# Pinning SyncE to the written plan, and leaving the instructions behind the second plan to the scheduler

## The chip, the cores and the metric

The kernel runs on one core of one Trainium2 chip. Five queues of instructions are spoken of: PE (TensorE matmuls; PEld are its weight loads), DVE (VectorE), ACT (ScalarE), POOL (GpSimd) and SP (SyncE, which in this kernel issues nearly every DMA transfer). The metric is the device time of one execution in microseconds (us); smaller is better. Each queue works through its own instructions strictly in the order in which the program holds them, and an instruction that waits for a semaphore holds all those behind it on its queue.

## The reference, cut to what matters

One decoder layer on x of 1024 tokens x 1024 columns in float32, with two inputs to one output projection and a gated feed-forward part with a short convolution:

```python
h = rms_norm(x, norm1_g)
q, k, v, glu_a, glu_b = split(h @ w_in)                 # 512 columns each
attn = stick_breaking_attention(rms(q), rms(k), v)      # 8 heads x 64
c = causal_depthwise_conv(glu_a * sigmoid(glu_b), conv_dw_w, conv_dw_b)   # 31 taps
c = silu(layer_norm(c))
x = x + concat([attn, c]) @ w_out
h = rms_norm(x, norm2_g)
gate, val = split(h @ w_up)                             # 2816 columns each
gate = silu(causal_depthwise_conv(gate, ffn_dw_w, ffn_dw_b))              # 3 taps
x = x + (gate * val) @ w_down
```

## The kernel before, in words

Everything is float32. A product of two float32 matrices is made of three matmuls (`mm3`, L386 to L389): each operand is split into a high part, a cast by ACT (L383), and a low part, a subtraction by DVE or POOL (L384 in `split`), and high x high (L387), high x low (L388) and low x high (L389) are summed in one PSUM bank. So before PE can start a product, ACT has to write the high part of a weight and another engine its low part.

The work has four stages, laid one over the other. First the input projection and the convolution module (until about 200 us of the profile), then the attention (about 200 to 400), then the output projection, the second norm and the transposed activations for the feed-forward part (until about 490), then `w_up` in 22 blocks of 128 gate and 128 value columns (until about 900) and `w_down`. Each `w_up` block f takes seven products instead of eight: the four quarters of its weights (a11, a12, a21, a22) and of the activations (b11, b21, b22) are combined into sums with the names S1 to S4 and T1 to T4, and the products 11·11, 12·21, S2·T2, S3·T3, S1·T1, S4·22 and 22·T4 are added up. A product is 12 matmuls over 512 columns, so a block is 84 matmuls.

For block f, `load_up(f)` has SP load two weight tiles (`rawu`, L1805, 512 KB each), and `sums_up(f)` makes the operands: POOL adds and subtracts quarters (s1 in L1829, a21 in L1830, a11 in L1831, a12 in L1835), ACT and DVE split the seven results. `up(f)` makes the products, adds them into the gate and value rows `gv` on DVE, makes the three-tap convolution (ACT L2009, two DVE operations L2011), the silu (ACT L2013) and the product with the value rows (DVE L2014), and has SP store the result (L2015, `act_d`).

What sets the order of the instructions: up to block 0 of `w_up`, the work is recorded as steps of a `Plan`, and `plan.run(ORDERS[0])` and `plan.run(ORDERS[1])` emit the steps in the order of two tables of numbers. The first table covers the work up to the attention and the output projection, the second the second norm, the transposes with the sums T1 to T4 (`both`, L1749 to L1751, and d1 to d4, L1783 to L1788) and the products of block 0 (`first_operands`, L1860 to L1947, among them L1885 for the low parts and L1928 for the sums into `gv`). A scheduler behind the kernel lays out all emitted instructions on the five queues by its own estimate of times. It keeps the emitted order only where `in_order` (L465) has tied each instruction of an engine to the one before it on that engine; the engines for which this is done are listed in `ORDERED` (L41): PE, DVE, ACT and POOL. SP is not among them, so the place of each DMA issue is the scheduler's choice.

`in_order` is called behind each of the two plans, and a third time in the loop over the blocks (L2023, when f is 0): there it also ties, on DVE, ACT and POOL, everything that was emitted by `load_up(1)`, `up(0)` and `sums_up(1)`, in the order in which the code is written. In that written order, the convolution, silu and gate product of block 0 come before the operands of block 1. Behind that the scheduler is free.

The names in the program have a number at the end that counts tiles; `aS_1_5097`, `aS_1_5100`, `aS_1_5103` and `aS_1_5107` are the parts of S2, S1, S3 and S4 of block 1, `a_1_5110` that of a22, `y_5086` is the gate of block 0, `aS_0_5018` is S4 of block 0 and `bT_4408` is T4.

Of the kernel before, what the change touches and what calls it, by code (L numbers as in the profile page):

```python
# [37 lines left out]
LN_AT = 190.0  # L38
PAIRS = [3, 2, 2, 2, 2]
AHEAD = 4  # L40
ORDERED = (mybir.EngineType.PE, mybir.EngineType.DVE, mybir.EngineType.Activation, mybir.EngineType.Pool)  # L41
AHEAD_Z, AHEAD_SCAN = 1.4, 0.5
QK_FROM, QK_TO = -3.0, 7.0
CONV_FROM, CONV_TO = 8.0, 31.0
# [100 lines left out]
class Plan:  # L145
# [36 lines left out]
    def add(self, cost, *args):  # L182
        if not isinstance(cost, dict):
            cost, args = {cost: args[0]}, (lambda eng, f=args[1]: f(),) + args[2:]
        op = Plan.Op()
        op.shares = "DVE2" in cost
        op.cost, op.emit, op.key = {e.rstrip("2"): c for e, c in cost.items()}, args[0], args[1]
        op.after = list(args[2]) if len(args) > 2 else []
        op.takes = list(args[3]) if len(args) > 3 else []
        op.end, op.engine, op.n, op.moves = None, None, len(self.ops), [Plan.ROWS]  # L190
        self.ops.append(op)
        return op
# [77 lines left out]
def kernel(  # L270
# [21 lines left out]
    nc = tc.nc  # L292
# [169 lines left out]
    def part_of(big_tile, i, words):  # L462
        return big_tile[:, i * words:(i + 1) * words]

    def in_order(start_at, last=None, engines=ORDERED):  # L465
        last = {} if last is None else last
        for ins in nc.cur_bb.bb.instructions[start_at:]:
            if ins.engine in engines:
                if ins.engine in last:
                    tc.add_manual_dep(ins, last[ins.engine].name, mybir.DependencyInfo(  # L470
                        mybir.DependencyClass.NoSync, mybir.DependencyReason.DATA), reason="planned order")
                last[ins.engine] = ins
        return last

    start_at = len(nc.cur_bb.bb.instructions)
    g1 = []
# [796 lines left out]
    for h, half in [(h, half) for h in range(H) for half in range(2)]:  # L1273
# [38 lines left out]
        for g in (2 * half, 2 * half + 1):  # L1312
# [47 lines left out]
            last = None  # L1360
            if g % 2 == 0:
                po, pd = plan.token("o"), {}
            for sp in range(g + 1):
# [50 lines left out]
                last = add("PE", 480, products, k, [c] + v2 + ([last] if last else [prev_last] if g % 2 else []))  # L1414
# [203 lines left out]

    plan.run(ORDERS[0])
    in_order(start_at)  # L1620
    conv_ctx.close()
    ps_ctx.close()
# [18 lines left out]
    start_at = len(nc.cur_bb.bb.instructions)  # L1641
# [154 lines left out]
    def load_up(f):  # L1796

        both = []
        for b in (0, DFF):
            if f == 1 and b == 0:  # L1800
                both.append(next_raw[0])
                continue
            both.append(op.tile([P, ND, P], F32, tag="xt", name=f"rawu{f}_{b}", bufs=3) if f % 2 else
                        raw([P, ND, P], F32, f"rawu{f}_{b}"))
            nc.sync.dma_start(both[-1], w_up_k[:, :, b + f * P:b + (f + 1) * P])  # L1805
        return both
# [177 lines left out]
    gv, banks_of, A_next, next_raw = [], {}, {}, []  # L1984
    first_operands(FIRST)
    plan.run(ORDERS[1])
    last_planned = in_order(start_at)
    start_at = len(nc.cur_bb.bb.instructions)

    def up(f, A):  # L1990
        def product(a, b):
# [25 lines left out]
    for f in range(NF):  # L2017
        if f + 1 < NF:
            raw_next = load_up(f + 1)
        up(f, A)  # L2020
        if f + 1 < NF:
            A = sums_up(f + 1, raw_next)
        if f == 0:  # L2023
            in_order(start_at, last_planned, ORDERED[1:])

# [117 lines left out]
    for i in range(len(PAIRS)):  # L2145
        for n, name in enumerate(using if i else making):
# [7 lines left out]
            for s in range(4):  # L2154
# [4 lines left out]
                for j, ((ah, al), (bh, bl)) in enumerate(parts):  # L2159
                    first, last = begins and j == 0, j == len(parts) - 1  # L2160
# [42 lines left out]
```

## Time and profile before

| | |
|---|---|
| median of 3 runs | 1114.94 us (1114.22 to 1115.05) |
| the profiled execution | 1115.21 us |
| its span in the trace | 1112.9 us |
| PE busy | 1088.1 us (98%) |
| DVE, ACT, POOL busy | 78%, 53%, 52% of the span |
| moved by DMA | 118.00 MB, 106 GB/s on average |

The span is the part of an execution between the first and the last instruction in the trace; 2.3 us of the profiled execution lie around it. Rows of the timeline read: start in us, duration in us, engine, line, operation, output<-input, shapes, how many were taken together, and in brackets the idle time of the engine before it and what ended that. Rows of the view of waits read: engine, output and line that waited, the releaser, total us, how many times, the longest. Rows of the windows read: the stretch, its length, then the busy time and number of instructions of PE, PEld, DVE, ACT and POOL, the clock granted to PE as a share of full speed, the share of the DMA engines' time and the GB/s moved.

### The profile page before, as it was taken

To read this page: it belongs to the slowest core of one execution; us is meant where nothing else is said; L and a number is where in the kernel's file an instruction comes from. 1 tells how busy PE (TensorE), PEld (TensorE's weight loads), DVE (VectorE), ACT (ScalarE), POOL (GpSimd) and SP (SyncE) were. 2 spreads that over 40 slices of the span, in tenths; PEclk is the share of its full clock that TensorE was granted. 3 is DMA by queue.
4 is the path that set the end of the run, shared out by engine and by line. 5 is a ranking of instruction groups with operands and counts; after the bars stand their busy time and mean duration, and the time that the engine had idled before them with its cause. 6 is when DMAs were issued, how large, how long until landed. Compare 5 with 4: busy or idle time off the path is not lost.

```text
span 1112.9 us, 14818 instructions
## 1 busy us (share of the span) xinstructions
PE 1088.1 (98%) x5258; PEld 905.4 (81%) x5258; DVE 871.7 (78%) x1200; ACT 586.9 (53%) x1050; POOL 580.6 (52%) x496
## 2 busy tenths in 40 slices
PE   8999999999999999979999999999999999999998
PEld 5888878889898887857888888888888888888887
DVE  5488798789989886878876777677777678797785
ACT  6445466676766654734433434333333378676660
POOL 3177889874734324753433133223322189888770
PEclk9999999999999999998999999999999999999999
DMA  7121210343732434522322222213132482403404
GB/s 269 39 57 32 82 58 20 114 152 120 238 87 77 142 122 144 171 57 78 112 79 92 77 95 75 96 62 107 59 96 75 149 324 77 150 21 133 152 2 150
DMA packets 110504, 118.00 MB, mean 106 GB/s; under 512 B 21369, under 2 KB 90208, under 8 KB 110430
## 3 DMA queue, kind: packets, MB, share of 16 engines
q1 hardware_dynamic: 110414, 117.06, 32.0%
q8 instruction: 41, 0.67, 0.3%
q14 instruction: 33, 0.27, 0.1%
q10 hardware_dynamic: 16, 0.00, 0.0%
HBM read 82.43 MB, written 28.31 MB: 100 GB/s over the span
## 4 chain that ended last, share of the span: by engine, by line
PE 86%; POOL 4%; DVE 3%; DMA 3%; ACT 2%; issue 2%; SPq 0%; DVEq 0%; POOLq 0%; ACTq 0%
PE dn L2162 19%; PE u_S L387 7%; PE u_S L388 7%; PE u_S L389 7%; PE u L387 5%; PE u L389 5%; PE u L388 5%; PE po L1403 3%; PE wT L1375 3%; PE qk L387 3%; PE qk L389 3%; PE qk L388 3%; POOL attn L879 2%; PE z L1334 2%; PE z L1335 1%
## 5 line engine op out<-in xcount | busy, mean ns | idle before, releaser
L2162 PE MATMUL dn<-wd,wd 128*128 128x512 f32 x768 | 181.4, 389 | 0.0
L2162 PEld LDWEIGHTS dn<-wd,wd 128*128 128x128 f32 x768 | 144.2, 188 | 29.9
L387 PE MATMUL u_S<-bT,aS 128*128 128x512 f32 x264 | 103.9, 393 | 10.4 <-ACT aS L383 10.4
L388 PE MATMUL u_S<-bT,aS 128*128 128x512 f32 x264 | 103.4, 392 | 0.0
L389 PE MATMUL u_S<-bT,aS 128*128 128x512 f32 x264 | 102.8, 390 | 0.0
L2165 DVE TENSOR_TENSOR c<-dn,c 128x512 f32<-128x512 f32 x120 | 81.5, 686 | 26.7 <-PE dn L2162 26.1
L2067 ACT CAST wd<-rawd 128x512 fp32r<-128x512 f32 x128 | 72.5, 619 | 32.8 <-DMA rawd<-act_d 9.5
L383 ACT CAST aS<-rawu 128x512 fp32r<-128x512 f32 x63 | 38.8, 621 | 93.2 <-PE u_S L389 66.9
L1356 DVE TENSOR_TENSOR_SCAN nb<-nb,one 128x128 f32<-128x128 f32 (+7 forms) x64 | 84.6, 1340 | 0.6 <-ACT nb L1342 0.5
L1829 POOL TENSOR_TENSOR s<-rawu 128x512 f32<-128x512 f32 x21 | 28.8, 1370 | 107.6 <-DMA rawu<-in_w_up_dram 80.8
L2066 ACT COPY whole<-rawd 128x512 f32<-128x512 f32 x110 | 63.4, 586 | 24.2 <-DVE wd L2068 11.6
L1835 POOL TENSOR_TENSOR rawu<-rawu 128x512 f32<-128x512 f32 x21 | 28.9, 1374 | 80.6 <-DVE a L384 80.6
L2068 DVE TENSOR_TENSOR wd<-whole,wd 128x512 fp32r<-128x512 f32 x90 | 59.9, 684 | 13.5 <-ACT wd L2067 6.7
L387 PEld LDWEIGHTS u_S<-bT,aS 128*128 128x128 f32 x264 | 50.0, 190 | 21.7 <-ACT aS L383 11.4
L2011 DVE SCALAR_TENSOR_TENSOR y<-gv,cols_a,y 128x1023 f32<-128x1023 f32 (+1 forms) x44 | 58.3, 1326 | 10.5 <-ACT y L2009 10.4
L383 ACT CAST a<-rawu 128x512 fp32r<-128x512 f32 x61 | 37.7, 621 | 54.3 <-PE u_S L389 33.9
L389 PE MATMUL u<-b,a 128*128 128x512 f32 x168 | 65.5, 390 | 0.0
L387 PE MATMUL u<-b,a 128*128 128x512 f32 x168 | 65.4, 389 | 0.0
L388 PE MATMUL u<-b,a 128*128 128x512 f32 x168 | 65.4, 389 | 0.0
L388 PEld LDWEIGHTS u_S<-bT,aS 128*128 128x128 f32 x264 | 50.1, 190 | 10.3
L389 PEld LDWEIGHTS u_S<-bT,aS 128*128 128x128 f32 x264 | 49.7, 188 | 10.4
L384 DVE TENSOR_TENSOR a<-rawu,a 128x512 fp32r<-128x512 f32 x61 | 45.4, 746 | 16.0 <-ACT a L383 16.0
(382 smaller groups left out, 3204.9 us busy)
## 6 DMA issues: line engine op xcount, KB each, us to landing
rawu<-in_w_up_dram SPq DMA_DIRECT2D x44, 512.0 KB
act_d<-y SPq DMA_DIRECT2D x22, 512.0 KB
rawd<-act_d SPq DMA_DIRECT2D x22, 512.0 KB
rawd<-in_w_down_dram SPq DMA_DIRECT2D x22, 512.0 KB
raw_qk<-in_w_in_dram SPq DMA_DIRECT2D x16, 256.0 KB
rawo<-in_w_out_dram SPq DMA_DIRECT2D x8, 512.0 KB
m<-conv_d SPq DMA_DIRECT2D x16, 256.0 KB
xt<-in_x_dram SPq DMA_DIRECT2D x8, 512.0 KB
```

The lines of the kernel that those rows point to most:

```text
L383: nc.scalar.copy(hi, src)
L384: lo_engine.tensor_tensor(lo, src, f32(hi), op=ALU.subtract)
L387: nc.tensor.matmul(ps, a_hi, b_hi, start=first, stop=False)
L388: nc.tensor.matmul(ps, a_hi, b_lo, start=False, stop=False)
L389: nc.tensor.matmul(ps, a_lo, b_hi, start=False, stop=last)
L1356: nc.vector.tensor_tensor_scan(rev, rev, ones_of[0][:, :w], 0.0, op0=ALU.mult, op1=ALU.max)
L2011: nc.vector.scalar_tensor_tensor(y[:, j:], g[:, :S - j], par("fw", (KF - 1 - j) * NF + f), y[:, j:], op0=ALU.mult, op1=ALU.add)
L2066: nc.scalar.copy(whole, src)
L2067: nc.scalar.copy(t[:, 0], src)
L2068: lo_engine.tensor_tensor(t[:, 1], whole, f32(t[:, 0]), op=ALU.subtract)
L2162: nc.tensor.matmul(ps, a[:, tok], b, start=first and m == 0, stop=last and m == 2, skip_group_check=True)
L2165: nc.vector.tensor_tensor(sums[c][s], ps, sums[c][s], op=ALU.add)
```

## The change

SP is added to the list `ORDERED`, so that both calls behind the two plans tie its DMA issues too, in the order in which the plans emitted them. And the third call of `in_order`, behind block 0's `up`, goes, with the parameters that only it needed; the instructions of `load_up(1)`, `up(0)` and `sums_up(1)` on DVE, ACT and POOL are then the scheduler's to place. (PE was not among the engines of that call.) No instruction is added or removed.

```diff
-ORDERED = (mybir.EngineType.PE, mybir.EngineType.DVE, mybir.EngineType.Activation, mybir.EngineType.Pool)
+ORDERED = (mybir.EngineType.PE, mybir.EngineType.DVE, mybir.EngineType.Activation, mybir.EngineType.Pool, mybir.EngineType.SP)
...
-    def in_order(start_at, last=None, engines=ORDERED):
-        last = {} if last is None else last
+    def in_order(start_at):
+        last = {}
         for ins in nc.cur_bb.bb.instructions[start_at:]:
-            if ins.engine in engines:
+            if ins.engine in ORDERED:
                 if ins.engine in last:
                     tc.add_manual_dep(ins, last[ins.engine].name, mybir.DependencyInfo(
                         mybir.DependencyClass.NoSync, mybir.DependencyReason.DATA), reason="planned order")
                 last[ins.engine] = ins
-        return last
...
     plan.run(ORDERS[1])
-    last_planned = in_order(start_at)
-    start_at = len(nc.cur_bb.bb.instructions)
+    in_order(start_at)
...
         if f + 1 < NF:
             A = sums_up(f + 1, raw_next)
-        if f == 0:
-            in_order(start_at, last_planned, ORDERED[1:])
```

Lines of the changed program are smaller by one behind L473, by two behind L1986 and by four behind L2022.

Three places show what moves. The first is ACT behind the second plan, at the step from block 0 to block 1. Before, the three operations on `y_5086` stand ahead of the five casts of block 1:

```order
L1881 CAST aS_0_5018<-rawu_0_4719 128x512
L1750 CAST bT_4408<-raws_4910 128x4x128
L383 CAST aS_2_5208<-s_2_5195 128x512
L2009 ACTIVATE y_5086<-gv,cols_a 128x1024
L2013 ACT_TABLE_LOAD
L2013 ACTIVATE y_5086<-y_5086 128x1024
L383 CAST aS_1_5097<-rawu_0_4868 128x512
L383 CAST aS_1_5100<-s_1_5093 128x512
L383 CAST aS_1_5103<-rawu_2816_5084 128x512
L383 CAST aS_1_5107<-rawu_0_4868 128x512
L383 CAST a_1_5110<-rawu_2816_5084 128x512
```

In the changed program:

```order
L1880 CAST aS_0_5018<-rawu_0_4719 128x512
L383 CAST aS_1_5100<-s_1_5093 128x512
L1749 CAST bT_4408<-raws_4910 128x4x128
L383 CAST aS_1_5103<-rawu_2816_5084 128x512
L383 CAST aS_1_5097<-rawu_0_4868 128x512
L383 CAST aS_1_5107<-rawu_0_4868 128x512
L383 CAST a_1_5110<-rawu_2816_5084 128x512
L383 CAST aS_2_5208<-s_2_5195 128x512
L2007 ACTIVATE y_5086<-gv,cols_a 128x1024
```

The five casts now stand ahead of `y_5086`, and the first of them ahead of the cast of T4; the five low parts on DVE move in the same way. The second place is POOL at the same point. Before, the sum s1 of block 1 and what follows from it stand behind the last planned low parts:

```order
L1885 TENSOR_TENSOR aS_0_4920<-s_0_4881,aS_0_4920 128x512
L1788 TENSOR_TENSOR raws_4910<-raws_4910,t_7_4935 128x512
L1751 TENSOR_TENSOR bT_4408<-raws_4910,bT_4408 128x4x128
L1885 TENSOR_TENSOR aS_0_5018<-rawu_0_4719,aS_0_5018 128x512
L1829 TENSOR_TENSOR s_1_5093<-rawu_2816_5084 128x512
L1830 TENSOR_TENSOR rawu_2816_5084<-rawu_0_4868,rawu_2816_5084 128x512
L1831 TENSOR_TENSOR rawu_0_4868<-s_1_5093,rawu_0_4868 128x512
```

In the changed program they are mixed in among those:

```order
L1884 TENSOR_TENSOR aS_0_4920<-s_0_4881,aS_0_4920 128x512
L1828 TENSOR_TENSOR s_1_5093<-rawu_2816_5084 128x512
L1787 TENSOR_TENSOR raws_4910<-raws_4910,t_7_4935 128x512
L1829 TENSOR_TENSOR rawu_2816_5084<-rawu_0_4868,rawu_2816_5084 128x512
L1750 TENSOR_TENSOR bT_4408<-raws_4910,bT_4408 128x4x128
L1884 TENSOR_TENSOR aS_0_5018<-rawu_0_4719,aS_0_5018 128x512
L1830 TENSOR_TENSOR rawu_0_4868<-s_1_5093,rawu_0_4868 128x512
```

Two operations of block 1 now stand ahead of the low part of T4, which PE needs for the last product but one of block 0. The third place is SP, from about 267 us into the run, between the first four heads of the attention and the last four. `attn<-q` and `late<-qk` copy a head's queries, twice side by side, for PE's transposes; `ahead` is a copy of the values shifted by one token; `rawo`, `m` and `xt` are operands of the output projection. Before:

```order
L1285 DMA attn<-q_1367 128x4x64 x4
L1461 DMA rawo_2741<-in_w_out_dram 128x1024
L1461 DMA rawo_2727<-in_w_out_dram 128x1024
L1550 DMA rawo<-in_w_out_dram 128x1024 x2
L1461 DMA rawo_2773<-in_w_out_dram 128x1024
L1461 DMA rawo_2753<-in_w_out_dram 128x1024
L1486 DMA m_2893<-conv_d_71 128x4x128
L1486 DMA m_2798<-conv_d_71 128x4x128 x2
```

In the changed program the last pair of `attn<-q` stands behind the four weight loads and two `m`, and the six `ahead` issues, which stood some 25 issues ahead of these rows (they were issued from 200 to 207 us), follow them:

```order
L1460 DMA rawo_2741<-in_w_out_dram 128x1024
L1460 DMA rawo_2753<-in_w_out_dram 128x1024
L1460 DMA rawo_2773<-in_w_out_dram 128x1024
L1485 DMA m_2798<-conv_d_71 128x4x128 x2
L1284 DMA attn<-q_1367 128x4x64 x2
L1485 DMA m_2893<-conv_d_71 128x4x128 x2
L1480 DMA xt_2948<-in_x_dram 128x1024
L651 DMA ahead_0_2992<-v_255 112x1024
L651 DMA ahead_0_2992<-v_255 15x1024
L652 DMA ahead_0_2992<-v_255 1x16x48
L651 DMA ahead_1_2993<-v_255 112x1024
L651 DMA ahead_1_2993<-v_255 15x1024
```

A pair of loads for the attention now waits behind larger loads, and six more issues lie ahead of the `late<-qk` loads. The rest of SP's moves are of the same kind and smaller: near the start, `raw_glu_b_303` (a weight tile of the input projection) moves from behind three `param_rows` loads and the last two `x_qk` loads to ahead of all five; at about 109 us, `raw_glu_a_1041` moves from among the `ends` and `ahead` issues of the first block of values to ahead of all of them. PE keeps its order up to the end of block 0, and then makes block 1's S2 and S3 products in two pieces each, where it had mixed the matmuls of S2, S3, S1 and S4.

## The prediction

> **What bounds the kernel now.** I read the page first, then PE's waits, then the timelines of all engines around the longest of them, then the windows, and last SP's issues against the first use of what they load. The page and the waits:
>
> ```profile
> PE 1088.1 (98%) x5258; PEld 905.4 (81%) x5258; DVE 871.7 (78%) x1200; ACT 586.9 (53%) x1050; POOL 580.6 (52%) x496
> ...
> PE u_S L387 <- ACT aS L383: 10.4, 1, 10.4
> PE v L739 <- DVE lo_v L604: 1.9, 1, 1.9
> ```
>
> PE is busy for 98% of the span, so the order of the other queues can matter only where PE waits. Two thirds of what PE waits for is a single wait, at the step from block 0 of `w_up` to block 1. PE's timeline there, then the windows:
>
> ```profile
> 490.02 0.39 PE L387 MATMUL u_S<-b,aS 128*128 128x512 f32 x1
> ...
> 492.51 0.39 PE L389 MATMUL u_S<-b,aS 128*128 128x512 f32 x1
> 503.33 0.79 PE L387 MATMUL u_S<-bT,aS 128*128 128x512 f32 x1 [10.43 <-ACT aS L383]
> ...
> 507.25 0.40 PE L389 MATMUL u_S<-bT,aS 128*128 128x512 f32 x1
> ```
> ```profile
> 490.00:500.00 10.00, 2.90 (x13) 2.06 (x11) 4.75 (x6) 1.86 (x2) 3.91 (x4) 0.83 0.15 40
> 500.00:510.00 10.00, 6.67 (x22) 5.08 (x23) 6.76 (x7) 4.93 (x7) 3.28 (x2) 0.65 0.26 87
> ...
> 520.00:700.00 180.00, 180.00 (x796) 149.10 (x795) 140.57 (x170) 68.14 (x98) 57.60 (x40) 1.00 0.28 88
> ```
>
> The first two rows are the first and the last matmul of block 0's S4 product, 12 matmuls that start 0.226 us apart (2.49 us over 11 steps). The third is the first of block 1. It is slow, and the clock granted in these 10 us is 0.65. From the start at 492.51 to that at 507.25 the trace has ten steps; at 0.226 us each they would take 2.26 us, and they took 14.74. So this place costs 12.5 us: 10.43 of waiting, and 2.0 of slow matmuls behind it. From 520 to 700 PE is busy for all 180 us at full clock; nothing behind the wait gives slack back, so what is saved here is saved at the end.
>
> Why PE waits is read from ACT and POOL:
>
> ```profile
> 494.10 0.62 ACT L383 CAST aS<-s 128x512 fp32r<-128x512 f32 x1 [9.96 <-POOL s L1829]
> 496.47 1.24 ACT L2009 ACTIVATE y<-gv,cols_a 128x1024 f32<-128x1024 f32 x1 [1.75 <-DVE gv L1928]
> 500.42 1.28 ACT L2013 ACT_TABLE_LOAD   x1 [2.71 <-DVE y L2011]
> ...
> 502.68 0.60 ACT L383 CAST aS<-rawu 128x512 fp32r<-128x512 f32 x1
> ```
> ```profile
> 481.66 1.83 POOL L1788 TENSOR_TENSOR raws<-raws,t 128x512 f32<-128x512 f32 x1
> 484.22 1.57 POOL L1751 TENSOR_TENSOR bT<-raws,bT 128x512 fp32r<-128x512 f32 x1 [0.73 <-ACT bT L1750]
> 485.76 1.74 POOL L1885 TENSOR_TENSOR aS<-rawu,aS 128x512 fp32r<-128x512 f32 x1
> 487.46 1.30 POOL L1829 TENSOR_TENSOR s<-rawu 128x512 f32<-128x512 f32 x1
> ...
> 490.21 1.29 POOL L1831 TENSOR_TENSOR rawu<-s,rawu 128x512 f32<-128x512 f32 x1
> ```
>
> POOL has the sums of block 1 ready at 491.5 us (490.21 and 1.29). ACT casts the first of them at 502.68, 11.2 us later, since its queue holds the convolution and silu of block 0 ahead of them; these wait for `gv`, and so for the last products of block 0. Nothing that PE needs next depends on them.
>
> **Part one: the third tie goes.** The order shows the five casts and the five low parts of block 1 ahead of `y_5086`. I rebuild the place by hand. POOL is free at 481.7 (row of 481.66). In the new order it does s1 (1.30, to 483.0), d4 (1.83, to 484.8), a21 (1.30, to 486.1), the low part of T4 (1.57, to 487.7), that of S4 (1.74, to 489.4) and a11 (1.29, to 490.7). ACT's cast of S2 then ends at 491.3 and its low part on DVE at 492.1 to 493; PE comes to it at 492.7. So the wait for the operands goes, or nearly.
>
> What is late next is the low part of T4, which has two more POOL operations ahead of it. PE's rows around it, and two of DVE:
>
> ```profile
> 487.30 0.39 PE L387 MATMUL u<-bT,a 128*128 128x512 f32 x1
> 487.53 0.39 PE L388 MATMUL u<-bT,a 128*128 128x512 f32 x1
> ```
> ```profile
> 482.26 1.78 DVE L1751 TENSOR_TENSOR bT<-t,bT 128x512 fp32r<-128x512 f32 x1
> 483.96 0.68 DVE L1885 TENSOR_TENSOR aS<-rawu,aS 128x512 fp32r<-128x512 f32 x1
> ```
>
> The second matmul of 22·T4 reads it at 487.53, 0.2 us before my estimate, and S4's is read at 490.25 or later, after 489.4. A DVE operation that lies beside a POOL one takes 1.78 instead of 0.68, and POOL's d4 beside it 1.83 instead of 1.30; if each of the two operations that were moved ahead loses such a half microsecond, PE waits 1.3. I take 0.6, nearer the end without collisions, because POOL's three durations that I used are already those with a collision; the bounds are 0 and 1.5. The term is 12.5 - 0.6 = 11.9 us saved, with ends 11.0 and 12.5.
>
> The Trainium skill, "SBUF — State Buffer", section "Who interferes with whom", speaks against this part: a VectorE operation with two SBUF inputs and a GpSimd operation that reads SBUF exclude one another for the whole of an instruction. The row of 482.26 agrees (0.68 of its own and about 1.1 of waiting). By that rule two moved operations that each lose a whole DVE operation of 0.68 make 1.4 us more, and the term would be 10.9 (an estimate).
>
> The convolution and silu move behind the casts. They free `gv` and PSUM banks for block 1; block 1 is 84 matmuls, or 19 us of PE, and ACT's five casts are 3.1 us at 0.62 (row of 494.10), so there is cover of over 10 us. The load for block 2, `rawu_0_5113`, waits for S4's low part of block 1, and this comes earlier with it. I cost both at nothing; without that cover, it would be the same wait one block later.
>
> **Part two: SP in the planned order.** Four places rest on loads.
>
> ```profile
> 11.07 1.06 SPq L512 DMA_DIRECT2D x_qk<-in_x_dram  x2
> ...
> 15.94 0.40 SPq L589 DMA_DIRECT2D raw_glu_b<-in_w_in_dram  x1
> ```
> ```profile
> 15.94 6.85 DMA raw_glu_b<-in_w_in_dram
> ```
> ```profile
> 22.88 1.23 DVE L611 TENSOR_TENSOR raw_glu_b<-raw_glu_b,gain 128x1024 f32<-128x1024 f32 x1 [3.26 <-DMA raw_glu_b<-in_w_in_dram]
> ...
> 24.62 1.41 DVE L604 SCALAR_TENSOR_TENSOR lo_v<-raw_v,gain,hi_v 128x512 fp32r<-128x512 f32 x2
> ```
>
> Start: `raw_glu_b_303` is issued at 15.94, lands 6.85 later (chain), and DVE stands 3.26 for it; behind it in DVE's queue is the `lo_v` that PE waits 1.9 us for. In the new order it stands where the second x_qk issue was, about 11.8, and by the same 6.85 it lands at 18.7. DVE's 3.26 and PE's 1.85 go. The last two x_qk loads land about 1 us later (two of their issues fill 1.06); I take it that this hides, and a rival takes the opposite. Bounds 0 and 1.9; I take 1.85, since 4 us earlier is more than the 3.26 that DVE stood.
>
> ```profile
> 109.15 0.57 SPq L589 DMA_DIRECT2D raw_glu_a<-in_w_in_dram  x1
> 109.78 1.60 SPq L652 DMA_DIRECT2D ahead<-v  x1
> ```
> ```profile
> 115.30 1.90 POOL L611 TENSOR_TENSOR raw_glu_a<-raw_glu_a,gain 128x1024 f32<-128x1024 f32 x1 [3.29 <-DMA raw_glu_a<-in_w_in_dram]
> ```
> ```profile
> 143.82 0.50 PE L387 MATMUL glu_a<-h_hi,hi_glu_a 128*128 128x512 f32 x1 [1.12 <-ACT cpad L827]
> ```
>
> At 109: POOL waits 3.29 us for `raw_glu_a`, and the chain runs from there over POOL to PE's 1.12 at 143.82. With the `ahead` issues behind it, the load has the queues to itself, and I estimate 2 us less for POOL. What stays between is all POOL work, which hands on between none and all of it: bounds 0 and 1.2, I take 0.6.
>
> From 267 to 310 the six `ahead` issues and the four `rawo` come in among loads that PE reads:
>
> ```profile
> 269.75 0.82 SPq L1461 DMA_DIRECT2D rawo<-in_w_out_dram  x2
> ...
> 273.48 3.82 SPq L1486 DMA_DIRECT2D m<-conv_d  x4
> 277.40 2.45 SPq L1481 DMA_DIRECT2D xt<-in_x_dram  x1
> ```
> ```profile
> 285.16 0.60 PE L1290 MATMUL qT<-ident_r,attn 128*128 128x128 f32 x4
> ```
> ```profile
> 306.38 0.63 PE L1290 MATMUL qT<-ident_r,late 128*128 128x128 f32 x4 [1.73 <-DVE diagonal L1391]
> ```
>
> The last pair of `attn<-q` is read by PE at 285.16. In the new order it is the seventh and eighth issue from 269.75. Issues that don't wait take 0.4 (two in 0.82), those of the `m` row 0.96 and the one at 277.40 took 2.45. At 0.96 the pair is issued by 277.4, and with 4 us to land (an estimate: a 512 KB load took 6.85 with the queues full, these are 128 KB each) it is there at 281.4, 3.7 us early. To the first pair of `late<-qk`, read at 306.38, it is 22 issues from 269.75; at 0.96 these and the landing end at 294.9, later if a store among them waits (next). Both hide; bounds 0 and the slower rival. A further load is `xt_3158`, which now stands behind a store and four `late` issues:
>
> ```profile
> 296.28 0.33 SPq L1522 DMA_DIRECT2D x_part<-xt  x1
> ```
> ```profile
> 305.85 1.27 POOL L1514 TENSOR_TENSOR xt<-prod,xt 128x512 f32<-128x512 f32 x1
> 310.39 0.62 POOL L1238 TENSOR_SCALAR keys<-qk 128x512 fp32r<-128x512 f32 x1 [3.28 <-PE kT L1255]
> ```
>
> The store waits for POOL's xt and cannot go before 296.3; behind it `xt_3158` is issued at 300 to 304 and lands at 304 to 309, and POOL reads it at 305.85. POOL stands for 3.28 us soon after, which absorbs most of up to 3 us. Bounds 0 and 2 us lost, I take 0.6.
>
> The Trainium skill, "DMA: Bandwidth & Descriptors", section "Anatomy of one DMA — SWDGE (gpsimd) path", says that the engines which move the data wait for no semaphore: any wait is on the sequencer that issues. That rule speaks against a pinned SP: a load behind a store that waits is not even queued. Before, the scheduler had put this load at 282.50, ahead of the store; the rule moves the sum by no more than the bounds just given.
>
> **The sum.** 1115.21 - 11.9 - 1.85 - 0.6 + 0.6 = 1101.5 us for an execution like the profiled one. That one lay 0.27 above the median of the runs, so I forecast 1101.2.
>
> **The rivals.** A: a wait takes the place of the one removed early on. The last two x_qk loads, now behind `raw_glu_b`, come late for the transposes, and PE stands for them instead; at 143.82 POOL's other work keeps the 1.12 as it is. Then part two brings nothing and costs 0.6: 1115.21 - 11.9 + 0.6 - 0.27 = 1103.6, or 1105 if `xt_3158` costs its 2 us. For it: all 3.3 us of DVE's stall came from loads that share the queues. Against: x_qk is only 1 us later.
>
> B: engines collide at the step to block 1. T4's low part is late by 1.5, PE stops, then waits another 1.5 for S2's parts behind DVE's queue, and the slow matmuls (2.0) come back: 11.9 becomes 12.5 - 5.0 = 7.5, and the time 1105.6. For it: 1.78 beside 0.68. Against: the operands have PE's 12 matmuls of S4 as cover.
>
> C, on the slower side: SP's issues choke. With the two mechanisms as in the sum, the 22 issues from 269.75 to the first `late` pair take x us each, and PE waits at 285.16 and 306.38, by 22x + 4 - 36.6 us in all, with 2.0 of slow matmuls behind each. This decides from x = 1.95, where it eats the 14.35 us of the three gains. At 2.45 for all, as the one issue at 277.40 took, it is 21.3 + 4.0 us, so 1115.21 - 14.35 + 25.3 - 0.27 = 1125.9. For it: the large loads at that place did slow SP. Against: the five issues of those two rows averaged 1.25.
>
> D: the change doesn't do what it says, PE's wait at 492 stays because another operand of block 1 is late by the same 10 us, and only the early gain comes: 1115.21 - 1.85 - 0.27 = 1113.1, within 0.2% of before. The order shows all five casts moved, so there is little for it.
>
> **How the numbers follow.** The forecast has 0.58, A 0.22, B 0.12, C 0.06, D 0.02. The forecast's own range is from all terms at their best (12.5 + 1.9 + 1.2 saved: 1099.3) to 1103. The range takes in A and B and their bounds: 1099.0 to 1106.5, which leaves out C and D and a little more. About 0.2% (2.2 us) is what a measurement of this kernel can tell from no change. Faster by more than that are the forecast, A and B, 0.92; within it D, 0.02; slower C, 0.06.
>
> **What would show it.** In the profile after: PE's wait for aS at the step to block 1 under 1.5 us and the granted clock of 490 to 510 near 1.00 (part one); POOL's T4 low part ending near 487.7 on the clock of before; `raw_glu_b` issued near 11.8 and no wait of PE for `lo_v` (A if one for hT has grown by as much); the wait of 1.12 for `cpad` half gone; the transposes of `attn` and `late` without a wait for DMA (C if one is over 5 us). The prediction is wrong if PE still stands over 4 us between blocks 0 and 1, or if waits above 2 us appear between 200 and 460 us.

## The result, and the profile after

The changed kernel takes 1097.73 us (median of 4 runs, 1097.61 to 1098.79), the kernel before 1114.99 beside it (4 runs, 1114.22 to 1116.24): 17.3 us less, a ratio of 0.9846 with a 95% interval of 0.9829 to 0.9863. I had forecast 1101.2 with a range of 1099.0 to 1106.5; the time lies 1.3 us below the range. The profiled execution took 1097.62 us with a span of 1095.8, so the two profiled executions differ by 17.6 us and their spans by 17.1. Two executions of the kernel before, made beside later runs, took 1367 and 3362 us at a granted clock of 0.75 and 0.32 and are in none of the comparisons.

First PE's row of the page of the changed kernel, then its view of PE's waits.

```profile
PE 1085.9 (99%) x5258; PEld 904.9 (83%) x5258; DVE 875.1 (80%) x1200; ACT 587.3 (54%) x1050; POOL 585.7 (53%) x496
```
```profile
PE hT L555 <- DVE x_k L548: 1.8, 1, 1.8
PE wT L1374 <- DVE tl L1395: 1.2, 1, 1.2
PE idle L483 <- DVE expo L350: 1.0, 1, 1.0
PE opa L387 <- ACT m L1682: 0.8, 1, 0.8
PE u_S L389 <- DVE aS L1884: 0.6, 1, 0.6
```

The wait of 10.4 us between block 0 and block 1 is gone, those for `lo_v` (1.9) and `cpad` (1.1) too, and so is one that the prediction did not count: PE's wait at 306 us. One of 0.6 us for a low part of block 0 is new.

PE's order is the same in both kernels up to block 1, and the number of matmuls is the same throughout. So the start of one matmul can be set beside the start of the same one in the other trace, and the difference read along the run. It changes in steps:

| first matmul behind the step (line of the kernel before) | before | after | difference | step |
|---|---|---|---|---|
| `hT` of x_q, L556 | 17.60 | 18.02 | +0.42 | +0.4 |
| `v`, L739 | 26.08 | 24.52 | -1.56 | -2.0 |
| `glu_a`, L387 | 143.82 | 140.94 | -2.88 | -1.3 |
| `z`, L1334 | 243.26 | 239.97 | -3.29 | -0.4 |
| `qT` of `late`, L1290 | 306.38 | 300.99 | -5.39 | -2.1 |
| `h2T`, L1738 | 470.21 | 464.52 | -5.70 | -0.3 |
| last but one product of block 0, L388 | 487.53 | 482.83 | -4.70 | +1.0 |
| last matmul of all | 1108.85 | 1091.79 | -17.06 | -12.4 |

The step to block 1 is worth 11.4 us (-12.4 and the +1.0 ahead of it), the pinned SP 5.7 us. The four views of the changed kernel at that step answer to those shown of before: PE's timeline, the windows, ACT and POOL.

```profile
479.97 0.50 PE L389 MATMUL u_S<-bT,aS 128*128 128x512 f32 x1 [0.64 <-DVE aS L1884]
...
482.39 0.39 PE L387 MATMUL u<-bT,a 128*128 128x512 f32 x1
482.83 0.50 PE L388 MATMUL u<-bT,a 128*128 128x512 f32 x1
...
487.95 0.39 PE L389 MATMUL u_S<-b,aS 128*128 128x512 f32 x1
488.17 0.39 PE L387 MATMUL u_S<-bT,aS 128*128 128x512 f32 x1
```
```profile
490.00:500.00 10.00, 10.00 (x46) 8.29 (x45) 9.14 (x9) 4.57 (x7) 6.07 (x5) 1.00 0.37 106
500.00:510.00 10.00, 10.00 (x46) 8.29 (x45) 10.00 (x12) 5.04 (x7) 4.74 (x3) 1.00 0.35 105
```
```profile
477.70 0.62 ACT L383 CAST aS<-s 128x512 fp32r<-128x512 f32 x1 [0.53 <-POOL s L1828]
...
486.20 0.62 ACT L383 CAST aS<-rawu 128x512 fp32r<-128x512 f32 x1 [4.48 <-POOL rawu L1830]
...
493.91 1.25 ACT L2007 ACTIVATE y<-gv,cols_a 128x1024 f32<-128x1024 f32 x1 [2.23 <-DVE gv L1927]
```
```profile
475.86 1.82 POOL L1828 TENSOR_TENSOR s<-rawu 128x512 f32<-128x512 f32 x1
477.63 1.73 POOL L1787 TENSOR_TENSOR raws<-raws,t 128x512 f32<-128x512 f32 x1
479.33 1.73 POOL L1829 TENSOR_TENSOR rawu<-rawu,rawu 128x512 f32<-128x512 f32 x1
481.02 1.75 POOL L1750 TENSOR_TENSOR bT<-raws,bT 128x512 fp32r<-128x512 f32 x1
...
484.43 1.74 POOL L1830 TENSOR_TENSOR rawu<-s,rawu 128x512 f32<-128x512 f32 x1
```

The last matmul of block 0 and the first of block 1 now start 0.22 us apart, and the granted clock is 1.00 where it was 0.83 and 0.65. ACT has the cast of S2 done at 486.8, and the silu of block 0 comes when its turn is. The price is in the first rows: 0.64 us of waiting for S2's low part of block 0 and about 0.2 (0.44 between two starts that else lie 0.23 apart) for that of T4, each with slow matmuls behind it. POOL's operations in these rows all take 1.73 to 1.82 instead of the 1.30 of one alone.

The wait that I had not counted is at 306 us. First SP in the changed kernel, then PE's transposes of the first `late` pair.

```profile
292.79 0.33 SPq L1521 DMA_DIRECT2D x_part<-xt  x1
296.48 2.79 SPq L1284 DMA_DIRECT2D late<-qk  x4
299.36 0.59 SPq L1480 DMA_DIRECT2D xt<-in_x_dram  x1
```
```profile
300.99 0.60 PE L1289 MATMUL qT<-ident_r,late 128*128 128x128 f32 x4
```

PE starts them with no wait, and it does so ahead of the DVE operation to which the view of before put its 1.73 us:

```profile
302.24 0.53 DVE L1390 TENSOR_TENSOR diagonal<-wT,diagonal 128x384 fp32r<-128x384 f32 x1
```

In the kernel before SP issued this pair at 301.63, behind a load of `xt` that it could not issue before 301.20; PE read it 4.8 us later, after 1.73 us of waiting:

```profile
301.20 0.33 SPq L1481 DMA_DIRECT2D xt<-in_x_dram  x1
301.63 6.70 SPq L1285 DMA_DIRECT2D late<-qk  x6
```

### The profile page after: what moved, and what is told of

It reads as the page before. It is cut to its first block, busy times and chain, and to the rows that moved or that the text cites. A ratio compares the mean times of both kernels' runs of the same rounds, so it can differ in the third digit from the quotient of the medians.

```text
span 1095.8 us, 14806 instructions
## 1 busy us (share of the span) xinstructions
PE 1085.9 (99%) x5258; PEld 904.9 (83%) x5258; DVE 875.1 (80%) x1200; ACT 587.3 (54%) x1050; POOL 585.7 (53%) x496
## 4 chain that ended last, share of the span: by engine, by line
PE 95%; DVE 1%; ACT 1%; DMA 1%; POOL 1%; issue 0%; SPq 0%; DVEq 0%; ACTq 0%; POOLq 0%
PE dn L2158 19%; PE u_S L387 7%; PE u_S L388 7%; PE u_S L389 7%; PE u L388 5%; PE u L389 5%; PE u L387 5%; PE po L1402 3%; PE wT L1374 3%; PE qk L387 3%; PE qk L389 3%; PE qk L388 3%; PE z L1333 2%; PE z L1334 2%; PE glu_a L387 1%; PE glu_b L388 1%
## 5 line engine op out<-in xcount | busy, mean ns | idle before, releaser
L388 PE MATMUL u_S<-bT,aS 128*128 128x512 f32 x264 | 102.7, 389 | 0.0
L387 PE MATMUL u_S<-bT,aS 128*128 128x512 f32 x264 | 102.7, 389 | 0.0
L2062 ACT COPY whole<-rawd 128x512 f32<-128x512 f32 x110 | 63.4, 585 | 24.5 <-DVE wd L2064 11.8
L2064 DVE TENSOR_TENSOR wd<-whole,wd 128x512 fp32r<-128x512 f32 x90 | 59.8, 682 | 11.8 <-ACT wd L2063 6.1
L388 PE MATMUL u<-b,a 128*128 128x512 f32 x168 | 65.4, 389 | 0.0
L387 PE MATMUL u<-b,a 128*128 128x512 f32 x168 | 65.3, 389 | 0.0
L389 PEld LDWEIGHTS u_S<-bT,aS 128*128 128x128 f32 x264 | 49.5, 188 | 11.4 <-DVE aS L1884 1.1
L387 PEld LDWEIGHTS u_S<-bT,aS 128*128 128x128 f32 x264 | 49.6, 188 | 10.3
L388 PEld LDWEIGHTS u_S<-bT,aS 128*128 128x128 f32 x264 | 49.5, 188 | 10.2
L1830 POOL TENSOR_TENSOR rawu<-s,rawu 128x512 f32<-128x512 f32 x21 | 31.4, 1495 | 47.4 <-DVE a L384 46.7
```

The costliest lines, as they stand in the source:

```text
L387: nc.tensor.matmul(ps, a_hi, b_hi, start=first, stop=False)
L388: nc.tensor.matmul(ps, a_hi, b_lo, start=False, stop=False)
L389: nc.tensor.matmul(ps, a_lo, b_hi, start=False, stop=last)
L2062: nc.scalar.copy(whole, src)
L2064: lo_engine.tensor_tensor(t[:, 1], whole, f32(t[:, 0]), op=ALU.subtract)
```

## The experiments

The theory behind the first four runs: the two halves of the change add up, and PE's wait at 306 us was for the load. Its rivals stand in the expectations.

**The third tie alone.** The kernel before without the call behind `up(0)`; SP stays the scheduler's. Every queue but SP then has the order of the changed kernel, and SP that of before but for one store (`act_d`), which goes behind the two `rawu` loads that stood behind it.

```diff
-        if f == 0:
-            in_order(start_at, last_planned, ORDERED[1:])
```

> Only the third tie is taken away; SP stays the scheduler's, as before. Theory (the two halves of the change are independent, each worth what the step of PE's starts shows): the step to block 1 gains 11.4 us, PE's waits of 1.9 for lo_v, 1.1 for cpad and 1.7 at 306 us stay: 1115.0 - 11.4 = 1103.6 us. Rival (the free order needs the loads of the pinned SP, for instance the operands of block 1 or 2 would come late): well under 10 us gained, over 1106, with a wait of PE for a rawu load or an operand of block 1 or 2.

Measured: 1103.25 us (4 runs, 1102.67 to 1103.55) beside 1115.16, ratio 0.9895 (0.988 to 0.991), 11.9 us less. In its view of PE's waits these two of the first 310 us are left:

```profile
PE glu_a L387 <- ACT cpad L827: 1.3, 1, 1.3
PE qT L1290 <- DVE nb L1356: 1.2, 1, 1.2
```

The theory holds for the time and for these two waits. The wait for `lo_v`, which it expected to stay too, is not there: in this execution PE had stood 2.0 us for `hT`, its starts were 2.0 us later than before by 11.5 us, and at 26 us, where the kernel before waits for `lo_v`, they are level again (0.1 later). The second row is the transpose of `late` again, and the releaser that the view names is now another DVE operation than before.

**SP alone.** `ORDERED` with SP, and the third tie kept on DVE, ACT and POOL:

```diff
+ORDERED = (..., mybir.EngineType.Pool, mybir.EngineType.SP)
-            in_order(start_at, last_planned, ORDERED[1:])
+            in_order(start_at, last_planned, ORDERED[1:4])
```

> SP is tied in both plans, and the third tie on DVE, ACT and POOL is kept. Theory: 5.7 us gained in the stretch up to 470 us, in three places (about 2.0 at 26 us, 1.3 at 144, 2.1 at 306, 0.3 at 470), and the wait of 10.4 between block 0 and block 1 as before: 1109.3 us. Rival (what was gained up to 470 us is mostly lost again at the step to block 1, since the wait there ends with a chain that does not get earlier): over 1112.

Measured: 1110.63 us (4 runs, 1108.37 to 1112.04), ratio 0.996 (0.9945 to 0.9975), 4.5 us less. PE's starts are 5.2 us earlier at 470 us, and the step to block 1 gives back 1.1 us of that: the wait is there and 10.7 long. The theory's 1109.3 us left this out.

```profile
PE u_S L387 <- ACT aS L383: 10.7, 1, 10.7
```

So 11.9 and 4.5 make 16.4 of the 17.3; the halves add up within what the runs spread.

**The late pair alone.** The kernel before, with one chain of ties on SP: the first four `late<-qk`, then the fifth `xt`. The numbers are places among SP's issues in the order of emission; the same helper serves the next two.

```diff
+    def sp_order(places):
+        issues = [ins for ins in nc.cur_bb.bb.instructions[start_at:] if ins.engine == mybir.EngineType.SP]
+        for p, q in zip(places, places[1:]):
+            tc.add_manual_dep(issues[q], issues[p].name, ...)
...
     in_order(start_at)
+    sp_order((107, 108, 109, 110, 125))
```

> The kernel before, with one thing tied on SP: the first four late<-qk issues go ahead of the fifth load of xt (xt_3507), which stands ahead of them before. Theory (PE's wait of 1.7 at 306.4 us, which the view puts down to a DVE operation, is in truth for the landing of the late load, issued at 301.6 behind xt_3507's): the wait goes, 2.1 us off PE's later starts, and the late load is issued about 4 us earlier. Rival (it is DVE's diagonal, as the view says): the wait stays at 1.7, whatever the load does.

Measured: 1113.42 us (10 runs, 1112.68 to 1113.95), ratio 0.9986 (0.9977 to 0.9996), 1.7 us less. SP's and PE's timelines:

```profile
300.03 2.69 SPq L1291 DMA_DIRECT2D late<-qk  x4
302.82 0.59 SPq L1487 DMA_DIRECT2D xt<-in_x_dram  x1
```
```profile
304.56 0.60 PE L1296 MATMUL qT<-ident_r,late 128*128 128x128 f32 x4
```

The pair went out 1.6 us earlier (I had expected 4), and PE's transposes start at 304.56 instead of 306.38 with no wait. Nothing else was moved, so the wait was for the load: this is shown.

**The load at 109 us alone.** The kernel before, with SP's issues from `raw_glu_b_987` to the last `ahead` of the first block of values in the order of the plan.

```diff
+    sp_order(range(33, 45))
```

> The kernel before, with one thing tied on SP: raw_glu_a_1041 goes ahead of all four ends and all six ahead issues, in the order of the plan. Theory: POOL's wait of 3.3 us at 112 us goes and all of PE's wait of 1.1 at 144 us, 1.3 us off PE's later starts. Rival (my first estimate: POOL's other work between keeps half of it): 0.6 us, with a wait for cpad of about 0.5 left.

Measured: 1113.37 us (10 runs, 1112.47 to 1114.61), ratio 0.9986 (0.9977 to 0.9995), 1.8 us less; PE's starts behind 144 us are 1.4 us earlier, and the wait for `cpad` is gone whole. Here the trace happened to name what `qT` waited for at 305 us:

```profile
304.69 0.63 PE L1296 MATMUL qT<-ident_r,late 128*128 128x128 f32 x4 [1.46 <-DMA late<-qk]
```

The same wait is put down to two different DVE operations in the traces of before and of the third tie alone, and to the load in this one.

**The start alone.** The kernel before, with SP's first 31 issues in the order of the plan.

```diff
+    sp_order(range(31))
```

> The kernel before, with one thing tied on SP: the issues up to the last param_rows load stand in the order of the plan, so raw_glu_b_303 goes ahead of the last two x_qk loads and of the param_rows. Theory: DVE's wait for raw_glu_b goes, PE's wait for lo_v (up to 1.9 us) goes with it, 1.0 to 2.0 us off PE's starts behind 26 us. Rival A of the prediction: the x_qk loads come late instead, PE's waits for hT grow by as much, nothing is gained behind 30 us.

Measured: 1114.22 us (10 runs, 1111.91 to 1115.85) beside 1114.74 (11 runs), ratio 0.9992 (0.9982 to 1.0002). In the profiled execution PE's starts are 2.1 us earlier behind 26 us, as expected, but the ten runs spread over 4 us and the gain is not clear of zero. So neither theory nor rival A as they stood: something in the start differs from run to run. Two later runs look at that.

**The tie on one engine alone.** The changed kernel with the third call put back, on ACT, on DVE or on POOL. Set against the kernel before, the edit is:

```diff
+ORDERED = (..., mybir.EngineType.Pool, mybir.EngineType.SP)
...
-            in_order(start_at, last_planned, ORDERED[1:])
+            in_order(start_at, last_planned, (mybir.EngineType.Activation,))   # or DVE, or Pool
```

> The changed kernel, with the third tie put back on ACT alone; DVE and POOL are the scheduler's. Theory (ACT's written order, silu of block 0 ahead of the casts of block 1, is enough to make the wait): PE's wait of about 10.4 for the casts is back, the time 12 us above the changed kernel, 1109 to 1110. Rival (the wait needs the tie on all three queues): under 5 us of waiting, under 1104.

Measured: 1113.08 us (one run). PE waits 10.6 us for ACT's cast, as before; PE's starts are 13.7 us later across the step than in the changed kernel. ACT's written order alone makes the wait. The time is 3 us above the 1110 expected: 1.7 us had been lost before 470 us, in an execution with 3.0 us of waiting for `hT`, and the step itself cost 13.7 where 12 was expected.

> The changed kernel, with the third tie put back on DVE alone. Theory: DVE's queue holds the five low parts behind the last operation of block 0's gate, so PE waits as long, but now for DVE's low part: 9 to 11 us, 1108 to 1110. Rival (ACT's queue alone was the cause, as the view of waits named it): the casts are early, so the wait is under 5 us, under 1103.

Measured: 1111.87 us (one run). With the casts early, PE now waits for DVE at that place, in two pieces:

```profile
PE u_S L389 <- DVE aS L384: 7.4, 1, 7.4
...
PE u L387 <- DVE gv L1928: 2.2, 1, 2.2
```

Together 9.6, and 12.3 us across the step: 7.4 for a low part, as expected, and 2.2 for a sum into `gv`, which stood on DVE behind an early low part of block 2. The rival falls: ACT's queue or DVE's alone is enough, though the view of before names ACT only. The time is 1.9 us above the 1110 expected, and 1.9 had been lost before 470 us, with 2.8 us of waiting for `hT`.

> The changed kernel, with the third tie put back on POOL alone: s1 and a21 of block 1 stand behind the low parts of T4 and S4 again. Theory (collisions of POOL and DVE at that place cost the changed kernel 1.0 us: 0.6 for S2's low part of block 0 and 0.4 for T4's): those two waits go, and block 1's S2 comes 0.5 to 1.2 late, so -0.5 to +0.2 against the changed kernel, 1097.2 to 1098.0. Rival (POOL's sums are needed where the scheduler put them): PE waits over 2 us for block 1, over 1099.5.

Measured: 1101.73 us (4 runs, 1099.57 to 1102.39), ratio 0.9878 (0.9859 to 0.9897). One half of the theory holds: both small waits are gone, and PE's starts are 1.1 us earlier across them than in the changed kernel. The other half does not: no operand of block 1 is late. PE makes the step with no wait at 489.13 us, and a wait that neither foresaw comes 22.5 us later, at 511.64 us, in the first product of block 2 that needs a sum, S2·T2:

```profile
PE u_S L389 <- DVE aS L384: 2.8, 1, 2.8
```

So the rival, a wait over 2 us for block 1, does not hold either, though the time came out where it had it. Across both blocks PE's starts gain 9.3 us instead of the changed kernel's 11.4; the scheduler's choice to pull two POOL operations ahead of T4's low part costs 1.1 us in block 0 and came out 2.1 better in all. Why block 2's S2 is late in the other order was not separated: POOL stood 4.4 us for a load at 500.1 us there, and DVE had the gate product ahead of the low part. The other 2.1 us of the time were lost before 470 us, with 2.8 us of waiting for `hT`.

**The changed kernel again, and with the start undone.** In the second kernel SP's first 31 issues are left untied, so the start is that of the kernel before.

```diff
-            if ins.engine in ORDERED:
+            if ins.engine == mybir.EngineType.SP and free:      # free = 31 for the first plan
+                free -= 1
+                continue
+            if ins.engine in ORDERED:
```

> The changed kernel as it is, timed again, because the profiles so far show that the first 14 us differ by up to 2 us from one execution to the next with the same order of loads: PE's wait for the third x_k load is 1.3 to 2.8 us, and behind a long one the first matmuls are slow. Theory: the changed kernel has lost the wait for lo_v that hid this, so its times spread by some 2 us, 1097.6 to 1100; the gain against the kernel before is 15 to 17 us. Rival (the spread is an affair of the other orders): 1097.5 to 1098.8 again.

> The changed kernel with SP's first 31 issues left to the scheduler, as in the kernel before; raw_glu_b_303 stands behind the x_qk loads and the first param_rows again. Theory: PE's wait for lo_v is back and ends where it ended before, whatever the first loads do: 0 to 2 us above the changed kernel, 1099 to 1100, with a smaller spread. Rival (the start part is worth its full 2.0 us in every execution): 2.0 us above the changed kernel's median, whatever that is.

Measured on the same chip: the changed kernel 1097.52 us (4 runs: 1100.70, 1096.82, 1098.22, 1096.77), ratio 0.9846 (0.983 to 0.9862); with the start undone 1099.35 (4 runs, 1099.15 to 1099.64), ratio 0.9858 (0.9842 to 0.9874). The spread is 3.9 us for the one and 0.5 for the other. The slowest of the changed kernel's runs was the profiled one; its windows at the start, then PE's wait:

```profile
8.00:12.00 4.00, 1.42 (x7) 1.42 (x8) 1.96 (x5) 3.01 (x6) 0.79 (x2) 0.67 1.08 384
12.00:16.00 4.00, 4.00 (x14) 3.33 (x13) 4.00 (x7) 4.00 (x8) 0.00 (x0) 0.50 1.05 388
```
```profile
PE hT L555 <- DVE x_k L548: 2.9, 1, 2.9
```

The third load of x_k, issued third in all these kernels, was read by ACT at 7.90 us in this execution and at 7.13 in the first profile of the changed kernel. PE waits 2.9 us for what follows from it instead of 1.8, and then has a clock of 0.50 to 0.67, so its starts are 2.9 us late by 13 us. In the kernel before and in that with the start undone, PE later stands for `lo_v`, which comes at a time set by the load of `raw_glu_b`; that wait swallows such a delay, as the run with the third tie alone showed (2.0 us late by 11.5 us, 0.1 at 26). The theory holds, with a spread twice what it expected: the term at the start is 2 us in a good execution and below zero in a bad one, and in the two medians here 1.8.

**More idle matmuls at the start.** The changed kernel, with PE kept busy for longer before the first transposes:

```diff
-            waits = [add("PE", 1280, lambda: pass_time(1, 3), T(at_), [g, w])]
+            waits = [add("PE", 1280, lambda: pass_time(1, 10), T(at_), [g, w])]
```

> The changed kernel with ten idle matmuls instead of three where PE passes the time until the first transposes, so that PE stands less while the third x_k load lands. Theory (the upper end of the changed kernel's spread, 1100.7, is a wait for hT of 2.5 us or more with slow matmuls behind it, as the granted clock of 0.50 to 0.67 from 8 to 16 us in that execution shows): PE's idle time there is shorter by the added 1.5 us, the clock stays near 1.00, and all executions lie at 1096.5 to 1098.5. Rival (the time is set by the landing of the load, the slow matmuls cost nothing extra): the spread stays, 1096.8 to 1100.7. Second rival: the added matmuls delay the first transposes and with them the chain over ACT, 0.5 to 1 us more in every execution.

Measured: 1098.45 us (5 runs, 1097.22 to 1099.04), ratio 0.985 (0.9837 to 0.9864). The profiled execution has a wait of 1.0 for hT and a clock of 1.00 from 4 to 20 us, and no run is over 1099.04, where the theory had 1098.5; but the median of the changed kernel's eight runs is 1097.74, so this is no better version, and with five runs it does not show that the slow ones are gone. The experiment is inconclusive between the theory and the second rival.

**The code in another order.** SP tied, the third tie kept on DVE, ACT and POOL, and `sums_up(1)` written ahead of `up(0)`:

```diff
-        up(f, A)
-        if f + 1 < NF:
-            A = sums_up(f + 1, raw_next)
+        if f == 0:
+            A_1 = sums_up(1, raw_next)
+            up(0, A)
+            A = A_1
+        else:
+            up(f, A)
+            if f + 1 < NF:
+                A = sums_up(f + 1, raw_next)
```

> SP is tied in both plans and the third tie is kept as before, but in the code sums_up(1) stands ahead of up(0), so the written order has block 1's operands ahead of block 0's convolution and silu. Theory (the written order was the fault, not the tie): the wait of 10.4 goes, but DVE's one early low part of block 2, for which its load is not there before 493 us, now stands ahead of block 1's low parts: a wait of 3 to 5 us is left, 1101.5 to 1104. Rival (any tie at that place costs the 10 us): 1108 or more.

Measured: 1100.78 us (one run), with 1.2 and 0.4 us of PE's waits left in block 1 and 0.4 in block 2; PE's starts gain 9.3 us there instead of the changed kernel's 11.4. The theory holds: DVE stood 4.15 us for that early low part of block 2 (it began at 489.75 us), and what this left of PE's waits was smaller than I had reckoned. The tie by itself did little harm here, 2.1 us; the order that it fixed did the rest. None of the kernels tried is clearly faster than the changed one.

## Why the prediction was wrong, point by point

The direction and the main mechanism were right, and none of the waits appears that were to show it wrong (over 4 us between blocks 0 and 1, over 2 us between 200 and 460 us). The size was too small by 3.6 us, 13.7 against 17.3, and that put the time below the range. By the terms of the sum:

- **The step to block 1: 11.9 forecast, 11.4 measured**, within its ends of 11.0 and 12.5. The late low part of T4 was foreseen, and 0.6 was its price. The runs show 1.0, of which the larger half fell on another low part, S2's of block 0 on DVE. The prediction's fence has that operation (483.96, 0.68 us), but I had not followed it: PE read it 0.4 us after its end. The sum had s1 and a21 on POOL at 1.30 us each; they took 1.82 and 1.73, and T4's low part ended at 482.77, which is 488.5 on the clock of before, not 487.7. That the total came out near is in part luck.

  The reading of the wait itself was not whole. It said that the silu waits for `gv` "and so for the last products of block 0". The chain that ends the wait begins with the load for block 2:

```profile
487.53 5.15 DMA rawu<-in_w_up_dram
```
```profile
494.75 1.08 DVE L384 TENSOR_TENSOR aS<-s,aS 128x512 fp32r<-128x512 f32 x1 [4.51 <-ACT aS L383]
495.76 0.68 DVE L1928 TENSOR_TENSOR gv<-u_S,gv 128x512 f32<-128x512 f32 x1
```

  From that load POOL made a sum of block 2 (492.81), ACT cast it (494.10), and its low part stood on DVE ahead of the sum of S4's product into `gv`, which began 2.9 us after that product's end (492.90). So two things stood ahead of block 1's operands: block 0's gate, by the written order, and ahead of the end of that gate one operation of block 2, whose place was the scheduler's. The second is what the last experiment kept.
- **The start: 1.85 forecast, 2.0 measured in the profiled execution.** That it came out near is luck: in the second profile of the same kernel PE is 1.5 us later at 26 us than in the kernel before. `raw_glu_b` went out at 12.54 instead of the 11.8 that I reckoned and was still early enough. Rival A had the right place, the first loads that share the queues, but the wrong load: it is the third of x_k. The change does not move it: SP's first fifteen issues are the same in all the kernels here, and two profiles of the changed kernel alone have it read at 7.13 and 7.90 us. What the change took away was the later wait that hid it.
- **The load at 109 us: 0.6 forecast, 1.3 measured.** I halved it because POOL has other work between. POOL began with this weight tile 4.9 us earlier than before, 3.3 of them since the load came sooner, and at its last operations ahead of `cpad` it was still 4.0 us earlier. So it handed on 2.4 us, and 1.1 was all that PE stood there. This is 0.7 of the missing 3.6.
- **The loads from 267 to 310: this is the step that failed.** The prediction said "Both hide; bounds 0 and the slower rival", and took 0. Its own fence held the row that speaks against this: PE's transposes of `late` at 306.38 with 1.73 us of waiting. I took the releaser in the brackets, a DVE operation, at its word. But no transpose needs that operation: in the changed kernel the transposes start at 300.99, 1.3 us ahead of the same DVE operation. The instruction waits for two loads as well as for DVE, and it was the load that came last. It measured 2.1 us in the table (1.9 at these transposes, the rest at 244 us, where PE's wait for `kT` fell from 0.5 to 0.3), and 1.9 with that pair alone moved.
- **`xt_3158`: 0.6 lost by forecast, nothing measured.** POOL does wait for it, 1.1 us, in a stretch where POOL has time.
- Steps of 0.4 at 243 and 0.3 at 470 us were not in the sum.

So 2.1, 0.7, 0.6 and 0.7 make 4.1 us that I missed, less 0.5 that I had too much at the step to block 1: about the 3.6 (the 0.4 lost in the first 18 us and the 0.15 at the start are left out). The low end of the range was all named terms at their best; it had no room for a term that was not named, and it should have had: the view of PE's waits before holds eight more rows, 7.3 us in all with the 1.7 for qT among them, of which the sum asked nothing. The prediction called the 10.4 us two thirds of what PE waits for; the rows add up to 20.7 us, so it is half.

Rival C, the choking of SP, found no support: the 17 issues from the first `rawo` to the last `ahead` took 16.4 us (266.47 to 282.82), 0.96 each, and PE waited for neither load. The rule of the Trainium skill on the port that VectorE and GpSimd share ("SBUF — State Buffer", section "Who interferes with whom") spoke against pulling POOL's work forward. In the changed kernel DVE's operations beside POOL's take 1.77 instead of 0.68 and POOL's 1.74 instead of 1.30, so the collision is there; its price of 1.0 us lies between my 0.6 and the 1.6 that the rule gave here (12.5 less 10.9). With POOL in its old order the price goes, but the 2.8 us of waiting in block 2 come, so the early start was worth its price.

## What to carry to other kernels

When a tie fixes the order of a stretch of code, look at which instructions of the next stage stand behind a long chain of the present one: here ACT's queue alone and DVE's alone were each enough to stop PE for 10 us, and the cure was the order, not the absence of the tie. A wait in the profile has one name, but an instruction may wait for several things; before a wait is left out of the sum, check that the named operation is one that the instruction reads or overwrites, and else look for the load. And a wait that is removed may have been hiding the jitter of something ahead of it: look at the spread of the times, not only the median.

## What the runs showed of the hardware that was not expected

- The time at which a load lands that shares the queues at the start differs from execution to execution with the same order of issues: the third x_k load was first read at 6.39 to 7.90 us in the fourteen profiles, in the two of the changed kernel at 7.13 and 7.90, while DMA moved 299 to 388 GB/s (4 to 16 us of the slowest).
- The granted clock fell behind quite short waits there. In the profiles with a wait for hT of 2.6 to 2.9 us (four) it was 0.50 to 0.65 from 12 to 16 us; with 2.0 to 2.3 us (six) it fell in three, to 0.69 to 0.74 in the lower of the stretches from 8 to 12 and from 12 to 16 us, and stayed 1.00 in the others; with 1.8 us or less (four) it stayed 1.00. The Trainium skill, "TensorE: Matmul & The Clock Gate", section "Part 1: The HAM clock gate (the "warmup" mystery)", puts the fall behind an idle window of about 3.4 us; here it came after less.
- In the changed kernel DVE and POOL work side by side from 476.45 to 481.6 us, both on operands in SBUF. DVE's three operations took 1.77 us each and POOL's 1.73 to 1.75, where they take 0.68 and 1.30 alone: both queues were slowed, not one of them.
